# RWKV scan of a flow-matching layer: two lanes of five chunks become two lanes of four and a third one of two

## The chip, the cores and the metric

The kernel runs on one core of a Trainium2 chip, in one launch. The metric is the device time of one execution in microseconds (us). The core has a matrix engine (PE), which reads its work in one fixed order, a vector engine (DVE), an activation engine (ACT), a general engine (POOL) and a queue (SP) that issues every DMA of this kernel. Matrix products are written to eight PSUM banks, from which DVE and ACT fetch them.

## The reference

One layer for two requests: 512 tokens of a sample and 128 tokens of a prompt. Input projection, then latent attention (8 heads) beside RWKV-7 time mixing (16 heads of 64), one output projection, a norm, a SwiGLU network and a second norm. The part that the change touches is the scan, which runs once forward and once backward, over the sample from given states and over the prompt from zero:

```python
def step(S, inp):
    r_t, w_t, k_t, v_t, kk_t, a_t = inp
    sa = jnp.einsum("bhvk,bhk->bhv", S, -kk_t)
    S = S * w_t[:, :, None, :] + sa[..., None] * (kk_t * a_t)[:, :, None, :] + v_t[..., None] * k_t[:, :, None, :]
    return S, jnp.einsum("bhvk,bhk->bhv", S, r_t)
```

and the adaLN modulation, which multiplies SiLU of two condition vectors by a matrix `w_mod` of 2048 x 12288:

```python
m = jax.nn.silu(cond) @ w_mod + b_mod
return jnp.split(m[:, None, :], 6, axis=-1)
```

## The kernel before

All 640 tokens lie side by side in the free dimension, 512 of the sample and then 128 of the prompt. The scan is cut into ten chunks of 64 tokens (`C`, `NCH`). Within a chunk it is a set of matrix products; from chunk to chunk a state of 64 x 64 for each head goes on. Heads are taken in pairs (`npairs` is 8), one head in each half of the 128 partitions.

A pair needs both directions over all ten chunks. It is done in two halves (`j` = 0, 1). In each half two **lanes** run side by side: the forward lane over five chunks and the backward lane over the other five. Each pair and half, sixteen in all and here called a phase, goes through the same stations, written as generators:

- `rwkv_prep` multiplies keys and receptances by the decays into `nk` and `pr` (DVE, POOL).
- `rwkv_grams` forms, for each chunk and head, the Gram product of `pr` and `nk`: one product of 64 x 128 weights a head, ten chunks in groups of four, four and two. ACT copies its quarters to `mab` and `mrb`, DVE masks the others into `pr` and, once at the end, `mrb`.
- `rwkv_turned`, a side job, turns the values `v` (one copy `vr` reversed in time) into `sv` and `zv` with 64 x 64 products against the identity, and `nk` into `bk`.
- `inverse` inverts the triangular 64 x 64 blocks of `mab`, mostly on DVE.
- `rwkv_chain` runs five **steps**. A step has four kinds of PE run: `px` (rows `m<-sv,pr`), copied to `xs` by ACT; the outputs of the step before (`m<-pr,sv` and `m<-mrb,zv`); `psg` (`m<-xs,uf`), copied to `zv` by ACT for one head and by DVE for the other; and `pn` (`m<-zv,bk`), which DVE turns into the next chunk's state with one SCALAR_TENSOR_TENSOR a lane and head (`sv<-m,dc,sd`; `sd` comes from POOL). The next `px` reads these states.

A prompt of two chunks is the head or the tail of a lane, so the lanes end, start or hand over in mid-chain; the table `AFTER` says where each state goes.

PE's order is not left to a scheduler. Every generator above, and the work that fills the gaps, is a `Job` with a rank; `Jobs.step` keeps a modelled PE clock, lets the job of the lowest rank that is ready issue, and a job that yields a number (`HOP["x"]`, `HOP["s"]`, `HOP["p"]` in the chain) is ready again after so much modelled time. The scan has rank 0. Below it stand the modulation products (`wmods`, rank 2), and the input projection (`main`, rows `acc<-xh,whi` and the like) or, when that has ended, attention. They fill what the scan leaves free. The other engines' order is chosen when the program is built.

The modulation columns that are not needed at once come through `wmod_ahead`: a megabyte of `w_mod` is loaded into the one buffer `wm4`, and four products (rows `x<-wm,cs`, 128 x 32 weights, 512 columns, four column groups of PE) are issued back to back; after `HOP["wm"]` the next four follow.

Of the kernel before, what the change touches and what calls it, by code (L numbers as in the profile page):

```python
# [46 lines left out]
for _n, _w in (("ident", 128), ("gmask", 128), ("lmask", 32), ("par", 2), ("blk", 128), ("cen", 128), ("blk2", 2), ("sel", 2),  # L47
               ("ones", 1), ("rst", 320), ("rot", 128)):
    CST[_n] = (_off, _w)
    _off += _w  # L50
# [110 lines left out]
def step_kernel(ctx: ExitStack, tc: tile.TileContext, a: dict, o: dict, upto: int = 99, npairs: int = NPAIR, dbg=None):  # L161
# [33 lines left out]
    def half(name):  # L195
        return rtile(name, HN, "h", 1)

# [209 lines left out]
    def token_shift(p0, p1, mi, mk=edge):  # L407
# [12 lines left out]
        return ((slice(0, NS), s[:, :NS]), (slice(NS, NT), s[:, 513:641]))  # L420
# [260 lines left out]
    def nat(d, j):  # L681

        h = j if d == 0 else 1 - j
        return slice(h * HN, h * HN + HN)

    def view(t, d, j):
        v = t[:, nat(d, j)]
        return v if d == 0 else v[:, ::-1]
# [25 lines left out]
    HV = [slice(0, HN), slice(HN, NT)]  # L714

    def rwkv_decays(i, j, sh):
# [3 lines left out]
        for d in range(2):  # L720
            col = 8 * d + i
            both = [(t, lw[:, c0 + d * P: c0 + d * P + P], x, r_, b, mps()) for t, c0, x, r_, b in
                    ((ld, 0, xw, slice(0, 64), w0_h), (ta, 256, xa, slice(64, 128), a0_h))]
            for t, w, x, r_, b, ps in both:
                T.matmul(ps[:, :HN], w, x[:, nat(d, j)], start=True, stop=False)

            for t, w, x, r_, b, ps in both:
                T.matmul(ps[:, :HN], w[r_], xl[r_, nat(d, j)], start=False, stop=True, share=0.5)
            for t, w, x, r_, b, ps in both:
                od = t[:, HV[d]] if d == 0 else t[:, HV[d]][:, ::-1]  # L730
                act(od, ps[:, :HN], AF.Tanh, bias=b[:, col: col + 1], scale=0.5)
            yield 2 * HOP["dec"]
        ts(V, ld, ld, -0.5 * EXPH, -0.5 * EXPH)
        for v_ in HV:
            V.tensor_tensor_scan(out=ld[:, v_], data0=con("rst"), data1=ld[:, v_], initial=0.0, op0=ALU.mult, op1=ALU.add)
# [6 lines left out]
        for d in range(2):  # L742
            stt(nb[:, HV[d]], ta[:, HV[d]], 1.0, view(kk, d, j), ALU.add, ALU.mult)
        ts(V, ta, ta, ka_h[:, i: i + 1], ka_c[:, i: i + 1])
        for d in range(2):
            tt(V, ta[:, HV[d]], ta[:, HV[d]], view(k, d, j), ALU.mult)
        for d in range(2):
            n_ = ks[:, nat(d, j)]
            src = ta[:, HV[d]] if d == 0 else ta[:, HV[d]][:, ::-1]
# [6 lines left out]
    def rwkv_prep(i, j, sh, u):  # L756
# [5 lines left out]
        for h in range(2):  # L762
# [3 lines left out]
            for d in range(2):  # L766
                es = slice(5 * d, 5 * d + 5)
                kv_, rv_ = (ch(t[rh, nat(d, j)]) for t in (kk, r))
                if d == 1:
                    kv_, rv_ = kv_[:, ::-1, ::-1], rv_[:, ::-1, ::-1]  # L770
                tt(V, pr[h][rh, es, 0, 1:C], kv_[:, :, 1:C], dd5[rh, es, 0:C - 1], ALU.mult)
                A.copy(pr[h][rh, es, 0, 0:1], kv_[:, :, 0:1])
                tt(G, pr[h][rh, es, 1, :], rv_, dd5[rh, es, :], ALU.mult)
        yield HOP["prep"] + (FIRST[1] if i + j == 0 else 0.0)

    def rwkv_turned(i, j, sh, u):

        nk, v = u["nk"], sh["v"]
        vr = half("vr")
        A.copy(vr, view(v, 1, j))  # L780
        sv_, zv, bk = u["sv"], u["zv"], u["bk"] = wide("sv"), wide("zv"), wide("bk")
        yield HOP["vr"]
        for d in range(2):
            src = v[:, nat(0, j)] if d == 0 else vr
            es = slice(5 * d, 5 * d + 5)
            ps = mps()
            for c in range(5):
                for h in range(2):
                    T.matmul(ps[hrow(h), cc(c)], src[rows(h), cc(c)], ident[rows(h), rows(h)], start=True, stop=True)
            for h in range(2):  # L790
                A.copy(sv_[hrow(h), es, h, :], ch(ps[hrow(h), :HN]))
                A.copy(zv[hrow(h), es, h, :], ch(ps[hrow(h), :HN]))
            yield HOP["tv"]
# [7 lines left out]
    def rwkv_grams(u):  # L801

        nk, pr = u["nk"], u["pr"]
        mab, mrb = u["mab"], u["mrb"] = ch(slot("mab")), ch(slot("mrb"))
        for e0, n in EG:
            es = slice(e0, e0 + n)
            both = [mps(), mps()]
            for e in range(n):

                for h, ps in enumerate(both):  # L810
                    T.matmul(ps[:, e * P: e * P + P], nk[rows(h), e0 + e].rearrange("p b t -> p (b t)"),
                             pr[h][rows(h), e0 + e].rearrange("p b t -> p (b t)"), start=True, stop=True, share=0.5)
            for h, ps in enumerate(both):
                ps4 = ps[:, :n * P].rearrange("p (c b t) -> p c b t", b=2, t=C)
                q = 1 - h
                A.copy(mab[rows(h), es], ps4[rows(h), :, 0, :])
                tt(V, pr[h][rows(q), es].rearrange("p c b t -> p c (b t)"),
                   ps4[rows(q)].rearrange("p c b t -> p c (b t)"),
                   con("gmask")[rows(q)].unsqueeze(1).broadcast_to([C, n, P]), ALU.mult)
                A.copy(mrb[rows(h), es], ps4[rows(h), :, 1, :])  # L820
            yield 2 * HOP["gram"]
        tt(V, mrb, mrb, con("gmask")[:, C:].unsqueeze(1).broadcast_to([P, NCH, C]), ALU.mult)
# [4 lines left out]
    AFTER = {(0, 0): ("next", "next", "next", "next", "carry"), (0, 1): ("next", "final", "next", "next", "carry"),  # L827
             (1, 0): ("next", "next", None, "next", "final"), (1, 1): ("next", "next", "next", "next", None)}

    def rwkv_chain(i, j, sh, u):  # L830

        sv_, zv, bk, mrb, pr, dc, cy = u["sv"], u["zv"], u["bk"], u["mrb"], u["pr"], u["dc"], sh["carry"]

        def lanes(t, h, e):

            return t[rows(h), e: e + 6: 5, h, :]
# [4 lines left out]
        if j == 0:  # L841
            sh["fs"] = rtile("fs", 2 * C, "fs", 2)
            sh["y"] = slot("y")
        for h in range(2):
            if j == 0:
                for d, e in ((0, 0), (1, 7)):
                    DMA.dma_start(out=sv_[rows(h), e, h, :], in_=a["states"][d, i, rows(h)])
                G.memset(sv_[rows(h), 5, h, :], 0.0)
            else:
                G.tensor_copy(lanes(sv_, h, 0), lane2(cy, h))  # L850
                G.memset(sv_[rows(h), 3, h, :], 0.0)
        y = sh["y"]

        def outputs(c):


            pss = [mps()[:, :C] for _ in range(2)]
            ms = (slice(0, C), slice(None, None, -1))
            for d, ps in enumerate(pss):
                for h in range(2):  # L860
                    T.matmul(ps[rows(h)], sv_[:, 5 * d + c, h, :], pr[h][:, 5 * d + c, 1, :][:, ms[d]], start=True, stop=False)
            for d, ps in enumerate(pss):
# [1204 lines left out]
```

## Time and profile before

| | us |
|---|---|
| median of 3 runs (lowest, highest) | 3418.34 (3415.4, 3426.62) |
| the profiled execution | 3418.1 |
| its span, first to last instruction | 3416.3 |
| scan, first Gram product to last output written | 207.7 to 1428.9 |
| last attention output written | 1433.0 |

| engine | busy us | share |
|---|---|---|
| PE | 3231.4 | 95% |
| DVE | 2489.4 | 73% |
| ACT | 1447.3 | 42% |
| POOL | 994.2 | 29% |

Up to 1434 us the scan is interleaved with the projection and then with attention; from there on only the output projection and the network run, which the change does not touch. In the rows of the profile "x8" counts records: a product in plain fp32 leaves two of them, one in the rounded format of the projections (fp32r) one. L115 is the one line through which nearly all products are issued, so groups are told apart by their tiles, written out<-in.

### The profile page before, as it was taken

The page shows a single profiled execution, that of the slowest core. Times are in us where ns is not written, and L with a number is a line of the kernel's source. Part 1 is how long each engine was busy: PE and PEld are TensorE (multiplying, and loading weights), DVE is VectorE, ACT ScalarE, POOL GpSimd, SP SyncE. Part 2 cuts the span into 40 slices and gives each one's busy share as a digit, 9 for nine tenths or more (in the row PEclk, how much of TensorE's full clock was granted, in tenths as well). Part 3 has the DMA queues.
Part 4 walks back from the last instruction along what each step waited for, and adds up shares of the span by engine and source line. Part 5 has one row for each costly group of instructions (what it writes and reads, how often), then busy time and mean ns, then how long its engine had stood idle before and what let it go on. Part 6 is the DMA issues. An engine that isn't in the chain of part 4 may idle for free.

```text
span 3416.3 us, 71056 instructions
## 1 busy us (share of the span) xinstructions
PE 3231.4 (95%) x27746; PEld 2973.9 (87%) x27746; DVE 2489.4 (73%) x4469; ACT 1447.3 (42%) x3028; POOL 994.2 (29%) x1034
## 2 busy tenths in 40 slices
PE   7999998999997988899989999999999999999998
PEld 3777777777876777799989999999999999999997
DVE  2466675666658666568688888888887769999677
ACT  1344343444444545445454444444444444333234
POOL 0012222222222222112265444444442332222124
PEclk9999998999998999999989999999999999999998
DMA  9755454542222110275434443344444367888643
GB/s 359 241 185 166 145 171 142 158 151 94 66 63 84 44 34 28 79 246 173 145 108 154 149 139 124 127 141 135 130 123 121 114 218 278 298 286 285 214 142 119
DMA packets 289344, 527.71 MB, mean 154 GB/s; under 512 B 30512, under 2 KB 76272, under 8 KB 289008
## 3 DMA queue, kind: packets, MB, share of 16 engines
q1 hardware_dynamic: 289008, 523.18, 46.7%
q8 instruction: 217, 3.56, 0.4%
q14 instruction: 119, 0.97, 0.1%
HBM read 428.99 MB, written 92.44 MB: 153 GB/s over the span
## 4 chain that ended last, share of the span: by engine, by line
PE 65%; DVE 8%; ACT 3%; issue 2%; DMA 2%; POOL 2%; SPq 0%; ACTq 0%; DVEq 0%; POOLq 0%
PE b L115 51%; PE acc L115 7%; PE m L115 5%; PE x L115 1%; DVE ql L229 1%; DVE pr L229 1%; POOL z L229 1%; DVE z L229 1%; DVE ip L229 1%; ACT z L241 0%; DMA z<-zd 0%; PE acc L119 0%; DMA k<-rkv 0%; DVE nk L238 0%; DVE wlo L229 0%
## 5 line engine op out<-in xcount | busy, mean ns | idle before, releaser
L229 DVE TENSOR_TENSOR ql<-raw,qh 128x512 fp32r<-128x512 f32 (+1 forms) x1064 | 888.6, 850 | 264.9 <-ACT qh L1307 250.6
L1307 ACT CAST qh<-raw 128x512 fp32r<-128x512 f32 (+1 forms) x1064 | 633.5, 610 | 831.0 <-PE b L115 643.2
L115 PE MATMUL b<-t,qh 128*128 128x320 f32 x2816 | 623.4, 310 | 8.3 <-ACT qh L1307 7.1
L229 POOL TENSOR_TENSOR raw<-raw,raw 128x512 f32<-128x512 f32 x240 | 351.8, 1466 | 807.1 <-DVE ql L229 561.2
L115 PE MATMUL b<-op,qh 128*128 128x320 f32 x2560 | 552.8, 311 | 2.0 <-DMA op<-hd 1.2
L115 PEld LDWEIGHTS b<-t,qh 128*128 128x128 f32 x2816 | 473.1, 189 | 9.6 <-ACT qh L1307 8.1
L115 PE MATMUL b<-p,qh 128*128 128x320 f32 x2112 | 469.5, 311 | 0.0
L115 PE MATMUL b<-t,ql 128*128 128x320 f32 x1408 | 436.2, 311 | 5.4 <-DVE ql L229 5.4
L115 PEld LDWEIGHTS b<-op,qh 128*128 128x128 f32 x2560 | 425.8, 189 | 4.0 <-ACT qh L1307 1.9
L115 PE MATMUL b<-op,ql 128*128 128x320 f32 x1280 | 378.9, 311 | 5.6 <-DVE ql L229 5.5
L115 PEld LDWEIGHTS b<-p,qh 128*128 128x128 f32 x2112 | 356.9, 190 | 0.1
L115 PE MATMUL b<-p,ql 128*128 128x320 f32 x1056 | 329.4, 312 | 6.1 <-DVE ql L229 6.1
L115 PE MATMUL acc<-xh,whi 128*128 128x320 f32 x1056 | 265.2, 333 | 9.7 <-ACT P L1170 3.9
L115 PEld LDWEIGHTS b<-t,ql 128*128 128x128 f32 x1408 | 265.3, 189 | 7.3 <-DVE ql L229 7.3
L115 PE MATMUL acc<-xh,wlo 128*128 128x320 f32 x1056 | 264.6, 333 | 4.8 <-DVE wlo L229 4.8
L115 PE MATMUL acc<-xl,whi 128*128 128x320 f32 x1056 | 261.5, 330 | 0.5 <-DVE xl L229 0.5
L115 PEld LDWEIGHTS b<-op,ql 128*128 128x128 f32 x1280 | 236.7, 189 | 8.4 <-DVE ql L229 8.2
L115 PE MATMUL b<-mh,qh 128*128 128x320 f32 x1024 | 230.2, 314 | 7.0 <-ACT qh L1307 6.0
L115 PEld LDWEIGHTS acc<-xh,whi 128*128 128x128 f32 x1056 | 180.8, 197 | 33.5 <-issue 12.7
L115 PEld LDWEIGHTS b<-p,ql 128*128 128x128 f32 x1056 | 200.1, 190 | 8.5 <-DVE ql L229 8.5
L229 DVE TENSOR_TENSOR wlo<-raw,whi 128x512 fp32r<-128x512 f32 (+1 forms) x161 | 110.3, 686 | 124.0 <-ACT whi L266 115.4
L115 PEld LDWEIGHTS acc<-xh,wlo 128*128 128x128 f32 x1056 | 180.6, 196 | 22.6 <-issue 9.2
(330 smaller groups left out, 5465.1 us busy)
## 6 DMA issues: line engine op xcount, KB each, us to landing
wm<-in_w_mod_dram SPq DMA_DIRECT2D x64, 1024.0 KB, 5.4
raw<-in_w_gate_dram SPq DMA_DIRECT2D x188, 256.0 KB, 2.7
raw<-in_w_up_dram SPq DMA_DIRECT2D x188, 256.0 KB, 2.9
op<-hd SPq DMA_DIRECT2D x136, 320.0 KB, 5.3
wm<-in_w_mod_dram SPq DMA_DIRECT2D x64, 512.0 KB, 7.5
raw<-in_w_out_dram SPq DMA_DIRECT2D x128, 256.0 KB, 2.9
raw<-in_w_down_dram SPq DMA_DIRECT2D x128, 256.0 KB, 5.4
raw<-in_w_in_dram SPq DMA_DIRECT2D x127, 256.0 KB, 2.7
```

The lines of the kernel that those rows point to most:

```text
L115: self.eng.matmul(out, lhsT, rhs, start=start, stop=stop)
L229: eng.tensor_tensor(out=out, in0=x, in1=y, op=op)
L1307: A.copy(hi, x)
```

## The change

- **Tokens are laid out anew** for the scan: the first 256 of the sample, the 128 of the prompt, the last 256 of the sample. A half `j` now has a segment of six chunks and one of four (`SEG`, `CHS`), one forward and one backward.
- **Three lanes, four steps.** In each half the two sample lanes take four chunks each, and the prompt's two chunks are a third lane that runs only in the first two steps (`lanes`). The products of all lanes of a step, outputs too, share one bank. ACT and DVE copy the third lane's part of `zv` with an instruction of its own each.
- **Gram products on quarters**: for each chunk and head two products with 64 x 64 weights in place of one with 64 x 128, sorted so that the quarters that go to `mab` and `mrb` for both heads lie in one bank; one ACT copy and one masked DVE copy fetch them.
- **Values move**: the reversed copy is made in `rwkv_prep`, and the turning of `v` follows the second and third Gram group at once instead of coming from the side job. The initial states are loaded in the side job.
- **Modulation** loads two megabytes into two buffers and issues eight products back to back, then waits 1.5 times as long. The space comes from a reserved area of on-chip memory that is cut to 1024 bytes.

The core of the diff:

```diff
     def wmod_ahead(n):
-        for k in range(0, KT, 4):
-            raw = hp.tile([P, 2048], F32, tag="wm4", name=nm("wm4"), bufs=1).rearrange("p (k c) -> p k c", k=4)
-            DMA.dma_start(out=raw, in_=a["w_mod"][n, k: k + 4].rearrange("k p c -> p k c"))
-            yield HOP["wm"]
-            for j in range(4):
-                yield raw[:, j]
+        for k in range(0, KT, 8):
+            raws = []
+            for q in (k, k + 4):
+                raw = hp.tile([P, 2048], F32, tag="wm4", name=nm("wm4"), bufs=2).rearrange("p (k c) -> p k c", k=4)
+                DMA.dma_start(out=raw, in_=a["w_mod"][n, q: q + 4].rearrange("k p c -> p k c"))
+                raws += [raw[:, j] for j in range(4)]
+            yield 1.5 * HOP["wm"]
+            yield from raws
...
+    SEG = (slice(0, 384), slice(384, NT))
+    CHS = (slice(0, 6), slice(6, NCH))
...
+        vr = u["vr"] = rtile("vr", 384, "h", 1)
+        A.copy(vr[:, :SEG[1 - j].stop - SEG[1 - j].start], sh["v"][:, SEG[1 - j]][:, ::-1])
...
+        sv_, bk = u["sv"], u["bk"]
+        for h in range(2):
+            if j == 0:
+                for d, q in ((0, 0), (1, 6)):
+                    DMA.dma_start(out=sv_[rows(h), q, h, :], in_=a["states"][d, i, rows(h)])
+                G.memset(sv_[rows(h), 4, h, :], 0.0)
+            else:
+                G.tensor_copy(sv_[rows(h), 2:7:4, h, :], cy[rows(h)].rearrange("p (d v) -> p d v", v=C))
+                G.memset(sv_[rows(h), 0, h, :], 0.0)
...
+        def values(g):
...
-                for h, ps in enumerate(both):
-                    T.matmul(ps[:, e * P: e * P + P], nk[rows(h), e0 + e].rearrange("p b t -> p (b t)"),
-                             pr[h][rows(h), e0 + e].rearrange("p b t -> p (b t)"), start=True, stop=True, share=0.5)
-            for h, ps in enumerate(both):
-                ps4 = ps[:, :n * P].rearrange("p (c b t) -> p c b t", b=2, t=C)
-                q = 1 - h
-                A.copy(mab[rows(h), es], ps4[rows(h), :, 0, :])
-                tt(V, pr[h][rows(q), es].rearrange("p c b t -> p c (b t)"),
-                   ps4[rows(q)].rearrange("p c b t -> p c (b t)"),
-                   con("gmask")[rows(q)].unsqueeze(1).broadcast_to([C, n, P]), ALU.mult)
-                A.copy(mrb[rows(h), es], ps4[rows(h), :, 1, :])
+                for h in range(2):
+                    for b in range(2):
+                        T.matmul(both[b != h][rows(b), e * P: e * P + P], nk[rows(h), e0 + e, b, :],
+                                 pr[h][rows(h), e0 + e].rearrange("p b t -> p (b t)"), start=True, stop=True, share=0.33)
+            pa, pb = (ps[:, :n * P].rearrange("p (c b t) -> p c b t", b=2, t=C) for ps in both)
+            A.copy(mab[:, es], pa[:, :, 0, :])
+            for h in range(2):
+                q = rows(1 - h)
+                tt(V, pr[h][q, es].rearrange("p c b t -> p c (b t)"), pb[q].rearrange("p c b t -> p c (b t)"),
+                   con("gmask")[q].unsqueeze(1).broadcast_to([C, n, P]), ALU.mult)
+            tt(V, mrb[:, es], pa[:, :, 1, :], con("gmask")[:, C:].unsqueeze(1).broadcast_to([P, n, C]), ALU.mult)
+            if n_:
+                values(n_ - 1)
             yield 2 * HOP["gram"]
-        tt(V, mrb, mrb, con("gmask")[:, C:].unsqueeze(1).broadcast_to([P, NCH, C]), ALU.mult)
...
+        def lanes(e):
+
+            return [q + e for q in first] + ([(4, 0)[j] + e] if e < 2 else [])
...
-        for e in range(5):
+
+        for e in range(4):
+            qs_ = lanes(e)
             px = mps()
-            for d in range(2):
+            for l, q in enumerate(qs_):
...
+            xs = rtile("xs", 3 * C, "xs", 2)
+            A.copy(xs[:, :len(qs_) * C], px[:, :len(qs_) * C])
...
             psg = mps()
-            for d in range(2):
+            for l, q in enumerate(qs_):
                 for h in range(2):
-                    T.matmul(psg[rows(h), cc(d)], u["u"][rows(h), cc(5 * d + e)], xs[rows(h), cc(d)], start=True, stop=True)
-            A.copy(lanes(zv, 0, e), lane2(psg, 0))
-            V.tensor_copy(lanes(zv, 1, e), lane2(psg, 1))
+                    T.matmul(psg[rows(h), cc(l)], u["u"][rows(h), cc(q)], xs[rows(h), cc(l)], start=True, stop=True)
+            A.copy(both(zv, 0, e), lane2(psg, 0))
+            V.tensor_copy(both(zv, 1, e), lane2(psg, 1))
+            if len(qs_) > 2:
+                A.copy(zv[rows(0), qs_[2], 0, :], psg[rows(0), cc(2)])
+                V.tensor_copy(zv[rows(1), qs_[2], 1, :], psg[rows(1), cc(2)])
             yield HOP["s"]
...
-                for d in ds:
-                    q = 5 * d + e
-                    dst = sv_[rh, q + 1, h, :] if to[d] == "next" else (cy if to[d] == "carry" else sh["fs"])[rh, cc(d)]
-                    stt(dst, pn[rh, cc(d)], dc[rh, q: q + 1], sd[rh, cc(d)], ALU.mult, ALU.add)
-            if e < 4:
+                for l in ls:
+                    dst = place(l, e)
+                    dst = dst[rh, h, :] if len(dst.shape) > 2 else dst[rh]
+                    stt(dst, pn[rh, cc(l)], dc[rh, qs_[l]: qs_[l] + 1], sd[rh, cc(l)], ALU.mult, ALU.add)
+            if e < 3:
                 yield HOP["p"]
...
-    nc = _bacc.Bacc("TRN2", target_bir_lowering=False, num_devices=1)
+    nc = _bacc.Bacc("TRN2", target_bir_lowering=False, num_devices=1, dynamic_dma_scratch_size=1024)
```

What the built programs hold, engine by engine, at three places. First PE, in the chain of half 0 of the second pair, from the products that end the outputs to the `pn` run (`m` is a PSUM tile, `xs`, `zv` and `bk` operands of the chain). Before, the third of five steps, with two lanes and one modulation burst of four:

```order
L115 MATMUL m_4467<-mrb_3762,zv_3952 64x64 x2
L115 MATMUL m_4468<-mrb_3762,zv_3952 64x64 x2
L115 MATMUL m_4479<-xs_4462,uf_162 64x64 x4
L115 MATMUL x_4006<-wm_750_4367,cs 32x512 x4
L115 MATMUL m_4492<-zv_3952,bk_3953 64x64 x4
```

The same chain after, the second of four steps:

```order
L115 MATMUL m_4509<-mrb_3822,zv_3819 64x64 x6
L115 MATMUL m_4525<-xs_4502,uf_162 64x64 x6
L115 MATMUL acc_4486<-xl_241,whi_4401 128x320 x2
L115 MATMUL acc_4486<-xh_240,wlo_4402 128x320 x2
L115 MATMUL acc_4486<-xh_249,whi_4401 128x320 x2
L115 MATMUL x_4162<-wm_725_4370,cs 32x512 x4
L115 MATMUL x_4162<-wm_726_4372,cs 32x512 x4
L115 MATMUL m_4552<-zv_3819,bk_3820 64x64 x6
```

Each run of the chain has six products in place of four in this step, and two modulation bursts stand together. Counted over the whole order up to the output projection, PE goes from a product on the full array (128 x 128 weights) to one on a part of it 388 times before and 319 times after. By the kind that follows: modulation bursts 64 and 47, values 27 and 0, runs of the chain 153 and 132, all others 144 and 140.

Second, DVE in the chain of half 0 of the third pair, from one copy of `zv` over the state updates (`sv`) to the next. Before:

```order
L900 COPY zv_5778<-m_6199 64x2x64
L238 SCALAR_TENSOR_TENSOR sv_5777<-m_6214,dc_5213,sd_6192 64x64 x4
L900 COPY zv_5778<-m_6253 64x2x64
L229 TENSOR_TENSOR wlo_6267<-raw_6171,whi_6266 128x512
L238 SCALAR_TENSOR_TENSOR sv_5777<-m_6274,dc_5213,sd_6238 64x64
```

After:

```order
L226 TENSOR_TENSOR wlo_6345<-raw_6217,whi_6344 128x512
L235 SCALAR_TENSOR_TENSOR sv_5653<-m_6310,dc_5329,sd_6269 64x64 x6
L235 SCALAR_TENSOR_TENSOR us_6330<-t_6329,mu_h,us_6330 128x641
L915 COPY zv_5654<-m_6386 64x2x64
L918 COPY zv_5654<-m_6386 64x64
L235 SCALAR_TENSOR_TENSOR sv_5653<-m_6405,dc_5329,sd_6365 64x64 x2
```

Six state updates stand together where four stood, and the third lane adds a copy of `zv` of its own (L918) behind that of the two sample lanes (L915).

Third, DVE at the end of the third pair's half 1 and the start of the fourth pair's half 0 (`pr` products of `rwkv_prep`; `y` are the chain's outputs). Before:

```order
L238 SCALAR_TENSOR_TENSOR sv_6691<-m_7303,dc_6040,sd_7273 64x64 x4
L229 TENSOR_TENSOR y_6178<-m_7328,y_6178 128x64
L229 TENSOR_TENSOR y_6178<-m_7329,y_6178 128x64
L900 COPY zv_6692<-m_7340 64x2x64
L229 TENSOR_TENSOR wlo_7408<-raw_7245,whi_7407 128x512
L238 SCALAR_TENSOR_TENSOR fs_6177<-m_7355,dc_6040,sd_7325 64x64 x2
L229 TENSOR_TENSOR pr_7374<-kk_6741,D_7029 64x5x63 x2
L229 TENSOR_TENSOR pr_7375<-kk_6741,D_7029 64x5x63 x2
L229 TENSOR_TENSOR y_6178<-m_7360,y_6178 128x64
L229 TENSOR_TENSOR y_6178<-m_7361,y_6178 128x64
```

After:

```order
L235 SCALAR_TENSOR_TENSOR sv_6581<-m_7403,dc_6195,sd_7363 64x64 x4
L226 TENSOR_TENSOR pr_7465<-kk_6872,D_7128 64x6x63
L226 TENSOR_TENSOR pr_7465<-kk_6872,D_7128 64x4x63
L226 TENSOR_TENSOR y_6259<-m_7426,y_6259 128x64 x2
L915 COPY zv_6582<-m_7437 64x2x64
L226 TENSOR_TENSOR pr_7466<-kk_6872,D_7128 64x6x63
L226 TENSOR_TENSOR pr_7466<-kk_6872,D_7128 64x4x63
L226 TENSOR_TENSOR y_6259<-m_7452,y_6259 128x64 x2
```

Two of the four `pr` products have moved ahead of the last step's `zv` copy, and the other two stand right behind it, so that fewer follow the end of the chain.

More of the change, by code (lines that the diff above doesn't have):

```diff
@@ L719, in rwkv_decays @@
         ld, ta = slot("ld"), slot("ta")
-        for d in range(2):
+        for g, sg_ in enumerate(SEG):
+            d = g ^ j
+            w_ = sg_.stop - sg_.start
             col = 8 * d + i
@@ L765, in rwkv_prep @@
             tt(V, nk[rh, :, 1 - h, :], ch(ta)[rh], ch(ld)[rh], ALU.mult)
[L766 to L769, printed above, removed]
+            for g, es in enumerate(CHS):
+                kv_, rv_ = (ch(t[rh, SEG[g]]) for t in (kk, r))
+                if g != j:
                     kv_, rv_ = kv_[:, ::-1, ::-1], rv_[:, ::-1, ::-1]
@@ L773, in rwkv_prep @@
                 tt(G, pr[h][rh, es, 1, :], rv_, dd5[rh, es, :], ALU.mult)
+        vr = u["vr"] = rtile("vr", 384, "h", 1)
+        A.copy(vr[:, :SEG[1 - j].stop - SEG[1 - j].start], sh["v"][:, SEG[1 - j]][:, ::-1])
         yield HOP["prep"] + (FIRST[1] if i + j == 0 else 0.0)
     def rwkv_turned(i, j, sh, u):
[L778 to L793, printed above, removed]
+        nk, cy = u["nk"], sh["carry"]
+        sv_, bk = u["sv"], u["bk"]
[7 more added lines that the diff above has]
+                G.memset(sv_[rows(h), 0, h, :], 0.0)
+        yield 0.4
         for e0, n in EG:
@@ L841, in rwkv_chain @@
+        gap = first[1] - first[0]
         if j == 0:
@@ L843, in rwkv_chain @@
             sh["y"] = slot("y")
[L844 to L859, printed above, removed]
+        y, fs = sh["y"], sh["fs"]
@@ new lines, in lanes, with both, lane2, place @@
+        def lanes(e):
+            return [q + e for q in first] + ([(4, 0)[j] + e] if e < 2 else [])
+        def both(t, h, e):
+            return t[rows(h), first[0] + e: first[1] + e + 1: gap, h, :]
+        def lane2(t, h):
+            return t[rows(h), :2 * C].rearrange("p (d v) -> p d v", v=C)
+        def place(l, e):
+            if l == 2:
+                return sv_[:, lanes(e)[2] + 1] if e == 0 else fs[:, cc(j)]
+            if e < 3:
+                return sv_[:, lanes(e)[l] + 1]
+            return cy[:, cc(1 - l)] if j == 0 else None
@@ L860, in outputs @@
+        def outputs(e):
+            qs_ = lanes(e)
+            ps = mps()
+            turned = [(q >= 6) != j for q in qs_]
+            for l, q in enumerate(qs_):
                 for h in range(2):
-                    T.matmul(ps[rows(h)], sv_[:, 5 * d + c, h, :], pr[h][:, 5 * d + c, 1, :][:, ms[d]], start=True, stop=False)
-            for d, ps in enumerate(pss):
+                    T.matmul(ps[rows(h), cc(l)], sv_[:, q, h, :], pr[h][:, q, 1, :][:, ::-1 if turned[l] else 1],
+                             start=l == 0, stop=False)
+            for l, q in enumerate(qs_):
@@ L863, in outputs @@
                 for h in range(2):
-                    T.matmul(ps[rows(h)], zv[rows(h), 5 * d + c, h, :], mrb[rows(h), 5 * d + c, :][:, ms[d]], start=False, stop=True)
-            for d in range(2):
-                yc = y[:, nat(d, j)][:, cc(c if d == 0 else 4 - c)]
+                    T.matmul(ps[rows(h), cc(l)], zv[rows(h), q, h, :], mrb[rows(h), q, :][:, ::-1 if turned[l] else 1],
+                             start=False, stop=l == len(qs_) - 1)
+            for l, q in enumerate(qs_):
+                c = q if not turned[l] else 15 - q if q >= 6 else 5 - q
+                yc = y[:, cc(c)]
@@ L955, in rwkv_post @@
             yield HOP["gup"]
-        DMA.dma_start(out=mix_d[8 + i], in_=y)
+        for out, src in ((slice(0, 256), slice(0, 256)), (slice(256, NS), slice(384, NT)), (slice(NS, NT), slice(256, 384))):
+            DMA.dma_start(out=mix_d[8 + i][:, out], in_=y[:, src])
     def rwkv():
```

108 lines of the change are left out of this document (55 added, 53 removed).

## The prediction

> **What bounds the kernel now.** First the chain of work that ended last, in its shares by engine, then the busy time by stage (columns: stretch, its length, busy PE, PEld, DVE, ACT, POOL with records, granted PE clock, DMA share, GB/s):
>
> ```profile
> PE 65%; DVE 8%; ACT 3%; issue 2%; DMA 2%; POOL 2%; SPq 0%; ACTq 0%; DVEq 0%; POOLq 0%
> ```
>
> ```profile
> 200.00:1050.00 850.00, 794.35 (x9698) 651.47 (x9698) 550.15 (x1211) 356.79 (x908) 190.53 (x324) 0.96 0.41 130
> 1050.00:1434.00 384.00, 334.69 (x3980) 290.91 (x3978) 261.78 (x600) 187.10 (x469) 93.75 (x141) 0.94 0.12 38
> 1434.00:1770.00 336.00, 309.05 (x1984) 300.25 (x1985) 253.33 (x410) 169.42 (x327) 101.10 (x87) 0.93 0.59 179
> ```
>
> The scan runs in the first two of these stretches. PE is busy there for 794 of 850 us (93%) and 335 of 384 us (87%); DVE for 65% and 68%. What follows 1434 us is untouched work behind the same fence, so the change is worth what it takes from the 1234 us of the scan. Which waits interrupt PE there, in total over that stretch (engine, tile, what it waits for: us, times, longest):
>
> ```profile
> PE m L115 <- DVE y L229: 22.1, 19, 2.7
> PE x L115 <- DVE ev L360: 8.1, 3, 6.1
> PE m L115 <- DVE zv L900: 6.5, 4, 4.1
> PE m L115 <- ACT pm L635: 6.3, 6, 2.7
> PE m L115 <- POOL sv L851: 6.0, 6, 1.2
> PE acc L115 <- ACT P L1170: 5.7, 4, 2.5
> PE m L115 <- DVE sv L238: 5.0, 2, 4.6
> ```
>
> Nothing large stands out: `zv`, `sv` and `xs`, the hand-overs within a chain, cost a few us over 80 steps. The gaps of the scan are filled by projection, modulation and attention, so **PE's own work sets the time**, and a shorter chain of latencies is worth little by itself. The terms below are therefore stretches of PE's row, from start to start.
>
> One step, near the middle of the first stretch, shows what a run costs (start, us, engine, line, out<-in, weights, shape, records):
>
> ```profile
> 571.10 0.56 PE L115 MATMUL acc<-xh,wlo 128*128 128x320 f32 x2
> 571.50 0.46 PE L115 MATMUL acc<-xh,whi 128*128 128x320 f32 x2
> 571.80 0.46 PE L115 MATMUL acc<-xl,whi 128*128 128x320 f32 x2
> 572.09 0.45 PE L115 MATMUL acc<-xh,wlo 128*128 128x320 f32 x2
> 572.48 0.45 PE L115 MATMUL m<-zv,bk 128*64 128x64 f32 x8
> 572.86 0.56 PE L115 MATMUL acc<-xh,whi 128*128 128x320 f32 x2
> ...
> 573.93 0.49 PE L115 MATMUL m<-sv,pr 128*64 128x64 f32 x8
> 574.22 0.44 PE L115 MATMUL m<-pr,sv 128*64 128x64 f32 x8
> 574.59 0.45 PE L115 MATMUL m<-mrb,zv 64*64 64x64 f32 x8
> 574.87 0.41 PE L115 MATMUL m<-xs,uf 64*64 64x64 f32 x8
> 575.21 0.42 PE L115 MATMUL acc<-xh,whi 128*128 128x320 f32 x1
> ```
>
> **1. Fewer alternations: −13.8 us.** A pair of projection records takes 0.295 us in the middle of a run (571.50 to 572.09 is two pairs in 0.59). The run of four pairs from 571.10 to 572.48 takes 1.38, not 4 x 0.295 = 1.18: going from the full array to a part of it and back costs 0.20 us. The order has 388 such changes before and 319 after: 69 x 0.20 = 13.8. This is pure PE time, beside nothing. Bounds: 0 if the 0.20 is a wait that merely moves, 13.8 if it is the array's.
>
> **2. Chain runs: −2.6 us.** A dropped step takes with it `px` 0.29 (573.93 to 574.22), outputs 0.37 + 0.28, `psg` 0.34 and `pn` 0.38: 1.66 us. For it ten runs (five kinds, two steps) grow from 8 records to 12. A record in a long run is read from the turning of values, 20 records in 0.73 us to the next run, against 8 in 0.28 for `m<-mrb,zv` above: 0.45 / 12 = 0.0375.
>
> ```profile
> 598.46 0.80 PE L115 MATMUL m<-cst,v 64*64 64x64 f32 x20
> 599.19 1.07 PE L115 MATMUL x<-wm,cs 128*32 128x512 f32 x8
> 600.18 0.80 PE L115 MATMUL m<-cst,vr 64*64 64x64 f32 x20
> ```
>
> So 10 x 4 x 0.0375 = 1.50 comes back: −0.16 a phase, −2.6 over 16. The records' number is the same in both kernels, so the bounds are 0 and, with half the runs' starts free, about −10.
>
> **3. Modulation bursts of eight: −3.2 us.** A burst of four products shows 8 records in two waves: the second starts 0.45 us after the first (568.75, 569.20), the next run 0.55 us after that (569.75).
>
> ```profile
> 568.75 1.07 PE L115 MATMUL x<-wm,cs 128*32 128x512 f32 x8
> 569.20 0.61 PE L115 MATMUL x<-wm,cs 128*32 128x512 f32 x4
> 569.75 0.51 PE L115 MATMUL m<-sv,pr 128*64 128x64 f32 x7
> 607.68 1.07 PE L115 MATMUL x<-wm,cs 128*32 128x512 f32 x8
> wm<-in_w_mod_dram SPq DMA_DIRECT2D x64, 1024.0 KB, 5.4
> ```
>
> Two bursts take 2 x 1.00 us; one of 16 records takes three waves at 0.45 and one at 0.55, 1.90: 0.10 saved, 32 times for the 64 loads of the last row. What could take it back is the load. One megabyte lands 5.4 us after its issue (last row: issues, size, median us to landing); of two, issued together when the burst before has freed both buffers, I estimate that the second lands some 3 us later, as they share the same engines. Bursts started as little as 8.5 us apart (599.19 to 607.68), of which the modelled wait is now half as long again, so that about 12 us lie between them and 1.9 + 5.4 + 3 fit. If one burst in three came 1 us late, it would be +10: bounds −3.2 and +10.
>
> **4. The third lane's waits: +9.6 us.** State updates follow one another on DVE, and `px` needs the last of them:
>
> ```profile
> 573.04 0.99 DVE L238 SCALAR_TENSOR_TENSOR sv<-m,dc,sd 64x64 f32<-64x64 f32 x4 [1.24 <-PE m L115]
> 571.22 0.26 ACT L899 COPY zv<-m 64x128 f32<-64x128 f32 x1
> 571.51 0.29 DVE L900 COPY zv<-m 64x128 f32<-64x128 f32 x1 [1.58 <-ACT zv L899]
> ```
>
> Four take 0.99, 0.25 each, and end at 574.03, when `px` (573.93) has begun: its last products already stand right behind the last update, with no slack. The modelled wait `HOP["p"]` ahead of `px` is as before. After step 0 there are six updates: +0.50, less 0.15 by which the longer `pn` (4 x 0.0375, counted in 2) pushes `px` back too: 0.35. After step 1 one update of the prompt stands ahead of the last that `px` needs: 0.25. Sum 0.60 a phase, 9.6 over 16. Behind a waiting `px` everything on PE is queued, so it is lost in full. Bound below: 0, if DVE starts on the first bank's products earlier.
>
> The third lane's `zv` adds a copy on ACT and one on DVE, and in these rows DVE's copy is released by ACT's of the same bank (571.22 + 0.26, start 571.51). If the two new ones follow in turn, that is 0.26 + 0.29 = 0.55 us more. `zv` is complete at 571.80 here and `pn` starts at 572.48: 0.68 us of projection products hides it, and I count it at 0. If that cover is gone it costs 0.55 x 2 steps x 16 = +17.6 (rival B), so the term's upper bound is +27.
>
> **5. DVE at the pair's end: −7.5 us.** Of the 22.1 us that PE waits for `y`, the Gram runs hold part:
>
> ```profile
> L115 PE MATMUL m<-pr,nk 64*128 64x128 f32 x640 | 55.4, 292 | 14.0 <-DVE y L229 7.5 <-POOL sv L851 6.0 <-ACT mrb L820 0.4
> 353.00 3.77 DVE L229 TENSOR_TENSOR pr<-kk,D 64x315 f32<-64x315 f32 x4
> 356.80 0.36 DVE L229 TENSOR_TENSOR y<-m,y 128x64 f32<-128x64 f32 x2
> 357.17 0.57 PE L115 MATMUL m<-pr,nk 64*128 64x128 f32 x5 [1.66 <-DVE y L229]
> ```
>
> Four `pr` products of the next pair, 3.77 us, stand on DVE between the chain's last update and its last `y`; the next Gram needs the banks that `y` holds and waits 1.66 us. All such waits are the 7.5 us of the group's row. In the new order two of the four products stand ahead of the last `zv`, and 3.77 / 2 = 1.9 us is more than 1.66, so the wait goes; next late there is POOL, whose 6.0 us stay. Bounds −7.5 and 0.
>
> **6. Gram products on quarters: 0.** A group of four chunks, 16 records, takes 1.09 us (585.92 to 587.01 below), 0.068 a record. The change doubles the records, each with weights of half the width.
>
> ```profile
> 585.92 1.16 PE L115 MATMUL m<-pr,nk 64*128 64x128 f32 x16
> 587.01 0.56 PE L115 MATMUL acc<-xl,whi 128*128 128x320 f32 x2
> ```
>
> If four quarters run side by side as two halves do now, 32 records take the time of 16 before. The nearest row is the turning of values, 64 x 64 products as well: 0.0375 a record, 32 of them 1.2 against 1.09, less by one change of kind. I take 0, as it is near that row. If only half of that runs side by side, each chunk costs (1.09 − 0.20) / 4 = 0.22 more, 160 chunks +35.
> The Trainium skill ("TensorEngine Tiling (Array Packing)", section "Restrictions and Gotchas", Gotcha 1) says that different row tiles cannot access the same PSUM bank simultaneously. Sorted quarters put both heads, that is both row halves, into one bank; by that rule they would take turns, and the sum would be +35 us higher (rival C). The trace speaks against it so far: `m<-cst,v` writes one bank from both halves and has 0.0375 us a record.
>
> **Covered.** ACT loses some 35 us of copies and DVE gets about 50 instructions more; ACT at 42% and DVE at 65% are hidden by PE, apart from term 4. Values moved into the Gram station are the same products on PE. The smaller reserved area gives only space.
>
> **Sum.** −13.8 − 2.6 − 3.2 + 9.6 − 7.5 + 0 = −17.5 us. The profiled execution took 3418.1 us, its span 3416.3; it lies 0.2 under the median of the runs shown (3418.34). From 3418.1: **3401 us**.
>
> **Rivals.** *A, the scan's path sets the end.* A step less saves 573.93 − 569.75 = 4.18 us of latency in each of 16 phases, 66.9, less 9.6: 3361. For it: 50 us idle in the second stretch. Against it: PE is 93% busy in the first, and the order ends the scan a few rows ahead of the last attention product. 6%.
> *B, the third lane's `zv` takes the place of what is gained.* No projection stands where its copies wait: −17.5 + 17.6, 3418, no change. It decides where less than 0.68 us of other products stands between the sample lanes' `zv` and `pn`. For it: ACT and DVE take turns on a bank in the row above. 20%.
> *C, Gram quarters take turns*, two at a time instead of four: 32 records at 0.068. Slower, 3401 + 35 = 3436. Half of that price, 0.051 a record, is where the gain is gone. Against it: the turning of values. 10%.
> *D, two megabytes come late*, more than the bound of term 3: also slower: with 1 us late in each of 32 bursts 3401 + 3 + 32 = 3436. 2%.
>
> **How the numbers follow.** Forecast 62%, A 6, B 20, C 10, D 2. About 0.3%, 10.3 us, is what a measurement of this kernel can tell from no change. Forecast bounds: with 1 at half its size, 4 at 17 instead of 9.6 and 5 at 0 the sum is +4; with 4 at 0 and 2 at its bound it is −34.5, 3422 and 3384 us. Of the forecast's 62, 52 are faster by over 10.3, 9 within, 1 slower; A is faster; of B 18 are within and 2 slower; C and D are slower. Faster 0.58, same 0.27, slower 0.15. The range takes in the forecast's own bounds with a little below them, B, and the part of C and D short of their full price: 3380 to 3434.
>
> **What would show it.** Step 1: shorter stretches of PE with the same waits; about 14 us fewer busy. 2 and 4: `px` of the second and third step starts behind the last of six and five updates, 0.35 and 0.25 us idle. 3: sixteen records in 1.90 us, none waiting for the load. 5: `y` gone from the waits of the Gram runs. 6: 32 records of a Gram group in 1.1 us; 2 us would be C. B would show as `pn` waiting for the third lane's copies. Wrong altogether would be an end of the scan set by a wait that the profile of before does not have.

## The result, and the profile after

The changed kernel takes 3387.34 us (median of 4 runs, 3386.45 to 3391.81) against 3416.87 us of the kernel before on the same chip: a ratio of 0.9914, 95% interval 0.9888 to 0.9939. That is 29.5 us less, where 17.5 were forecast; 3401 was predicted with a range of 3380 to 3434, so it lies inside, on the fast side. Run again beside the experiments, the changed kernel gave 3384.58 us, ratio 0.9910 (0.9894 to 0.9926).

First the busy time by stage of the changed kernel (columns as before). The stage that the change does not touch begins 34 us earlier (first product of the output projection at 1403.9 us instead of 1438.0) and takes 1982 us instead of 1978; over all runs it takes 1974 to 1983:

```profile
200.00:1050.00 850.00, 787.28 (x10442) 660.59 (x10438) 579.50 (x1305) 335.00 (x837) 210.87 (x348) 0.96 0.40 133
1050.00:1404.00 354.00, 310.97 (x3912) 276.41 (x3911) 238.17 (x562) 163.15 (x407) 90.43 (x137) 0.96 0.13 37
1404.00:1740.00 336.00, 311.51 (x2004) 302.84 (x2005) 254.65 (x412) 169.37 (x327) 101.20 (x88) 0.94 0.58 177
1740.00:3385.00 1645.00, 1622.30 (x10950) 1610.46 (x10948) 1339.30 (x2089) 679.32 (x1217) 590.80 (x440) 0.99 0.52 173
```

Then five groups of instructions on PE from 200 to 1404 us, whose idle time (last columns: us before them, and what ended it) the readings below use:

```profile
L115 PE MATMUL m<-pr,nk 64*64 64x128 f32 x1280 | 49.7, 277 | 12.8 <-DVE pr L226 10.6 <-DVE mrb L226 2.2
L115 PE MATMUL m<-sv,pr 128*64 128x64 f32 x640 | 43.1, 243 | 3.5 <-DVE sv L235 3.4
L115 PE MATMUL m<-zv,bk 128*64 128x64 f32 x576 | 37.4, 238 | 13.9 <-DVE zv L915 5.4 <-DVE zv L918 4.2 <-ACT zv L914 3.1
L119 PE MATMUL m<-cst,nk 128*128 128x128 f32 x160 | 27.0, 285 | 9.9 <-ACT bk L791 5.4 <-DVE ks L226 4.0 <-DVE y L963 0.4
L115 PE MATMUL x<-cst,ev 128*128 128x2 f32 x120 | 15.6, 252 | 1.3 <-DVE ev L359 1.3
```

and the same groups of the kernel before (200 to 1434 us; the Gram row is in the prediction):

```profile
L115 PE MATMUL m<-sv,pr 128*64 128x64 f32 x640 | 42.3, 244 | 5.1 <-DVE sv L238 5.0
L115 PE MATMUL m<-zv,bk 128*64 128x64 f32 x576 | 37.5, 241 | 8.0 <-DVE zv L900 6.5 <-DVE y L229 1.0 <-ACT zv L899 0.4
L119 PE MATMUL m<-cst,nk 128*128 128x128 f32 x160 | 26.4, 281 | 0.0
L115 PE MATMUL x<-cst,ev 128*128 128x2 f32 x120 | 16.2, 257 | 8.1 <-DVE ev L360 8.1
```

Waits have changed places: the copy of the modulation sums (`ev`) no longer holds PE, but `pn` waits 5.9 us more for `zv`, and the transposes that make `bk` (`m<-cst,nk`) wait 9.9 us where they waited for nothing. Groups that are not shown moved as much: `m<-u,pm` from 6.4 to 1.4 us, `acc<-kh,qh` from 6.3 to 1.1, `m<-ks,cst` from 0 to 5.0.

The busy times of these rows overlap one another on PE, and part of them ran at half the clock (140 us before the output projection in the trace of before, 110 in this one). So PE's work was also added up from its records' starts: from each record to the next one's start (or to its own end, where PE then idles), halved where the granted clock was 0.50, up to the output projection's first product. Beside it stand the time lost to the half clock and the idle time. Halving is a little too much: a projection pair takes 0.533 us at 0.50 and 0.294 at full clock, which makes some 1 us between two rows of the table. One profiled execution each, us:

```text
                          projection  modul.  Gram  chain  rest   work   lost at 0.50  idle
before                       530.4    107.7   51.1  138.3  411.7  1239.1     60.0      131.0
changed                      516.1    104.2   43.4  138.8  414.8  1217.4     47.3      131.4
changed, again (e1)          515.0    101.0   43.7  138.8  413.5  1212.1     51.6      131.8
Gram on halves (e2)          516.0    102.9   49.4  137.8  416.6  1222.7     46.0      129.2
bursts of four (e3)          517.4    107.4   42.8  138.8  415.3  1221.9     36.5      123.6
no third lane (e4)           526.2    101.8   47.9  140.6  412.6  1229.2     48.4      125.8
later px (e5)                517.8    102.8   42.4  133.4  416.2  1212.5     44.9      123.6
before, bursts of 8 (e9)     528.8    102.7   51.7  140.3  414.4  1237.8     46.9      120.0
later px, four (e12)         516.6    108.7   42.3  129.9  416.1  1213.7     45.2      135.2
```

"Chain" is the five kinds of chain run. The columns projection, Gram and chain repeat within about 1 us between two executions of the changed kernel, modulation within some 3. PE's work falls by 21.7 and 27.0 us, 24 on average, and the idle time stays. In the first pair of traces work, half clock and idle time together fall by 34 us. The 12.7 us less at half clock in the first pair of traces are hardly the change's: the profiled execution of before had a mean clock of 0.969, below its usual one. Over 43 runs of the kernel before (one more, at a clock of 0.866, is left out as disturbed) and 8 of the changed one the mean granted clock is the same, 0.972.

### The profile page after: what moved, and what is told of

Same layout as the page of the kernel before. It is cut to its first block, busy times and chain, and to the rows that moved or that the text cites. A ratio compares the mean times of both kernels' runs of the same rounds, so it can differ in the third digit from the quotient of the medians.

```text
span 3385.6 us, 72312 instructions
## 1 busy us (share of the span) xinstructions
PE 3198.5 (94%) x28386; PEld 2964.2 (88%) x28386; DVE 2486.0 (73%) x4520; ACT 1398.1 (41%) x2890; POOL 1006.4 (30%) x1050
## 4 chain that ended last, share of the span: by engine, by line
PE 73%; DVE 11%; DMA 3%; ACT 3%; issue 3%; POOL 1%; SPq 0%; ACTq 0%; DVEq 0%; POOLq 0%
PE b L115 51%; PE acc L115 11%; PE m L115 8%; PE x L115 2%; DVE z L226 1%; DVE pr L226 1%; DMA wm<-in_w_mod_dram 1%; DVE ql L226 1%; DVE wlo L226 1%; DMA k<-rkv 1%; DVE ip L226 1%; POOL z L226 1%; PE acc L119 0%; DVE nk L226 0%; ACT z L238 0%
## 5 line engine op out<-in xcount | busy, mean ns | idle before, releaser
L115 PE MATMUL acc<-xh,wlo 128*128 128x320 f32 x1056 | 256.7, 325 | 3.2 <-DVE wlo L226 3.2
L263 ACT CAST whi<-raw 128x512 fp32r<-128x512 f32 (+1 forms) x161 | 95.8, 595 | 246.8 <-PE acc L115 197.3
```

The source lines that it names most:

```text
L115: self.eng.matmul(out, lhsT, rhs, start=start, stop=stop)
L263: A.copy(hi, r)
```

## The experiments

Each is compared with the changed kernel's ratio to the kernel before, 0.9910 (0.9894 to 0.9926), by its own ratio; 0.001 is 3.4 us.

**e1, the changed kernel again.**

> The changed kernel once more, to compare the next three with on one chip. The gain over the kernel before is 29.5 us by the medians (17.5 forecast). If part of it is the granted clock (110 us at half speed before the scan's end here, 137 in the kernel before), another profile of the same kernel may show 120 to 140 us at half speed and a time some 5 to 10 us longer. If the stretches at half speed belong to the program, it shows about 110 again.

Measured 3384.58 us. Half speed before the scan's end: 124 us, against 110 in the first execution. The stretches vary from one execution to the next, so a single pair of traces doesn't tell the clock's share.

**e2, the Gram products on halves again.**

```diff
-                    for b in range(2):
-                        T.matmul(both[b != h][rows(b), e * P: e * P + P], nk[rows(h), e0 + e, b, :],
-                                 pr[h][rows(h), e0 + e].rearrange("p b t -> p (b t)"), start=True, stop=True, share=0.33)
+                    T.matmul(both[h][:, e * P: e * P + P], nk[rows(h), e0 + e].rearrange("p b t -> p (b t)"),
+                             pr[h][rows(h), e0 + e].rearrange("p b t -> p (b t)"), start=True, stop=True, share=0.528)
```

> The changed kernel with the Gram products as one of 64 x 128 weights a head again (the banks then hold one head each, so ACT and DVE fetch the diagonal quarters with two copies instead of one); the order on PE is as in the changed kernel otherwise. If the quarters are worth what the starts on PE show (52 us of pitch before, 43 after), 6 to 12 us slower than the changed kernel. If they cost nothing, as the prediction had it, the same within 3 us. If they take turns by the bank, faster by up to 35 us.

Measured 3386.43 us, ratio 0.9919 (0.9905 to 0.9934): 3 us slower by the ratios, with an uncertainty of some 6. In the table the Gram column rises by 5.9 us. PE's timeline, first a group on quarters in the changed kernel, then one on halves in e2 (start, us, ..., records):

```profile
504.49 0.46 PE L115 MATMUL acc<-xh,wlo 128*128 128x320 f32 x2
504.87 1.92 PE L115 MATMUL x<-wm,cs 128*32 128x512 f32 x16
506.73 1.10 PE L115 MATMUL m<-pr,nk 64*64 64x128 f32 x32
507.66 0.86 PE L115 MATMUL m<-cst,v 64*64 64x64 f32 x24
```

```profile
654.60 1.16 PE L115 MATMUL m<-pr,nk 64*128 64x128 f32 x16
655.70 0.56 PE L115 MATMUL acc<-xh,wlo 128*128 128x320 f32 x2
```

32 records take 506.73 to 507.66, 0.93 us, where the values follow at once, and 1.03 us in the undisturbed groups that a projection product follows; 16 on halves take 1.09 to 1.10, whatever follows them, values or projection. Quarters of both heads that share a bank, each head's row half writing 64 partitions of its own there, do not take turns: the prediction's price for that was 0.22 us for each of four chunks, 0.88 us more. This is where the trace answers the rule on row tiles and PSUM banks that the prediction weighed ("TensorEngine Tiling (Array Packing)", "Restrictions and Gotchas", of the Trainium skill): for this pattern no such cost shows.

**e3, bursts of four from one buffer in the changed kernel** (the function `wmod_ahead` of before).

> The changed kernel with modulation bursts of four out of one buffer. By terms 1 and 3 of the prediction: 17 changes of kind more at 0.20 us and 32 x 0.10 us of waves, 6.6 us slower. If a change of kind costs nothing in the end, 0 to 3 us slower; if the second megabyte comes late in the changed kernel, faster.

Measured 3370.27 us, ratio 0.9877 (0.9859 to 0.9895): 11 us *faster* by the ratios and 14 by the medians. Faster had been expected only if the second megabyte came late, and it does not: PE waits for `wm` 1.3 and 0.0 us in the two traces of the changed kernel, and 5.2 us here. PE's work is 4.5 to 9.8 us more, as terms 1 and 3 have it, but 8 us less is idle and 11 to 15 us less is lost at half clock. The clock is no accident of one execution here: 0.977 to 0.979 in all four runs, 0.970 to 0.974 in the eight of the changed kernel.

**e4, the change without the third lane**: the kernel before, its Gram function's products and copies as in the change, bursts of eight. The new layout of the tokens and the moved values are missing with the lane.

> The kernel before (two lanes of five chunks, values turned by the side job) with the Gram products on quarters and the bursts of eight, so that the third lane alone is missing from the change. If PE's own work decides, it is slower than the changed kernel by what lanes save in changes of kind and runs: about 47 changes at 0.20 us and 2.6 us, less the waits, 5 to 15 us. If the scan's path sets the end, nearly the whole gain is in the lanes: 22 us or more.

Measured 3394.97 us, ratio 0.9948 (0.9931 to 0.9965): 10 to 13 us slower than the changed kernel. This is PE's own work: 11.8 to 17.1 us more in the table, 10 to 11 of it projection products, which stand in 361 runs here and in 288 there. How much of that is the lane's and how much the moved values' was not separated.

**e5, later `px`.**

```diff
-                yield HOP["p"]
+                yield HOP["p"] + (0.35, 0.25, 0.0)[e]
```

> The changed kernel with the modelled wait ahead of px longer by 0.35 us after step 0 and by 0.25 us after step 1, so that projection products are ordered into the waits for the six and five state updates. By term 4 of the prediction (9.6 us of such waits) some 5 to 10 us faster than the changed kernel; by the trace after (3.4 us of waits of px for sv) the same within 3 us.

Measured 3363.44 us, ratio 0.9855 (0.9836 to 0.9874), 19 to 21 us faster than the changed kernel and 1.45% faster than the kernel before: the lowest of all, though its interval overlaps that of e3. PE's timeline at the `px` after step 0 (12 records), first in e1, then in e5:

```profile
702.83 0.83 PE L115 MATMUL m<-sv,pr 128*64 128x64 f32 x11
703.39 0.27 PE L115 MATMUL m<-pr,sv 128*64 128x64 f32 x1
703.49 0.22 PE L115 MATMUL m<-sv,pr 128*64 128x64 f32 x1
```

```profile
702.72 0.45 PE L115 MATMUL acc<-xh,whi 128*128 128x320 f32 x2
703.11 0.57 PE L115 MATMUL m<-sv,pr 128*64 128x64 f32 x12
703.50 0.52 PE L115 MATMUL m<-pr,sv 128*64 128x64 f32 x12
```

From the first to the last record it is 0.66 us in e1 (to 703.49) and typically 0.35 in e5; after step 1, 0.49 and 0.23. So 0.31 + 0.26 = 0.57 us a phase is a wait for the last state update, 9.1 us over 16, and it hides *inside* the run: the column of idle time shows only 3.5 us for `px`. In the table the chain loses 5.4 us, and 3.4 of idle before `px` go as well: 8.8 us. But PE's whole work, 1212.5 us, is no less than in e1 (1212.1), as projection, modulation and the rest take more; against e1 it is idle time (8 us) and half clock (7 us) that fall. So the 9.1 us are shown in the `px` runs, not in the kernel's time.

**e6, the `pr` products segment by segment.** The loops over heads and segments change places in `rwkv_prep`.

> The changed kernel with the pr products on DVE written segment by segment instead of head by head, so that the first Gram group has all it needs after two or three of the four products. The Gram runs wait 10.6 us for pr in the changed kernel: if that wait is on the path that sets the time, 4 to 9 us faster; if something else is late next at the same place (y, POOL), the same within 3 us.

Measured 3386.21 us, ratio 0.9923 (0.9907 to 0.9940), the same or slightly slower. The Gram runs' wait fell from 12.8 to 6.8 us:

```profile
L115 PE MATMUL m<-pr,nk 64*64 64x128 f32 x1280 | 50.2, 277 | 6.8 <-DVE pr L226 5.3 <-DVE mrb L226 1.4
```

PE's whole idle time in the trace fell by 4.6 to 5.0 us, but not the time of the kernel. Six us at 6 places are below what this comparison tells.

**e7 and e8, an unused product among the projection's.**

```diff
             yield from mm3(ps, w, k * P, xs[kt], kt == 0, kt == len(xs) - 1)
+            if k == 1 and len(xs) == KT and g % 2 == 0:
+                T.eng.matmul(ps[0:64, 0, 400:464], ident[0:64, 0:64], con("ident")[0:64, 0:64], start=False, stop=False)
```

e8 has `ps[:, 0, 400:464], ident, con("ident")[:, 0:64]`. 56 such products each.

> The changed kernel with one unused fp32 product of 64 x 64 weights and 64 columns in every second granule of the input projection, between two projection products, into unused columns of their bank. In the trace the pitch around it is the cost of going to a part of the array and back: 0.20 us by term 1 beside its own two records. If the cost belongs to what stands around a chain run and not to the array, there is none here beyond its records (some 0.08 us).

> The same with 128 x 128 weights. If 0.20 us is for the array's division, the pitch around it has nothing beyond its own two records (some 0.08 to 0.15 us). If it is for the change of number format (fp32r to fp32), it is as large as with the 64 x 64 product.

PE's timeline, first e7, then e8:

```profile
656.23 0.46 PE L115 MATMUL acc<-xh,wlo 128*128 128x320 f32 x2
656.62 0.33 PE L287 MATMUL acc<-cst 64*64 64x64 f32 x2
656.88 0.56 PE L115 MATMUL acc<-xh,whi 128*128 128x320 f32 x2
657.27 0.46 PE L115 MATMUL acc<-xl,whi 128*128 128x320 f32 x2
```

```profile
653.23 0.46 PE L115 MATMUL acc<-xh,wlo 128*128 128x320 f32 x2
653.53 0.33 PE L287 MATMUL acc<-cst 128*128 128x64 f32 x2
653.66 0.54 PE L115 MATMUL acc<-xh,whi 128*128 128x320 f32 x2
654.04 0.46 PE L115 MATMUL acc<-xl,whi 128*128 128x320 f32 x2
```

From the projection pair ahead to the second pair behind, e7 takes 656.23 to 657.27, 1.04 us, and e8 653.23 to 654.04, 0.81. Both hold four projection records (0.59). So the product on a quarter costs 0.45 us and the one on the full array 0.22: **0.23 us is for going to a part of the array and back**. In 23 undisturbed places of each trace the two stretches take 1.04 and 0.80 to 0.81 us. Something also remains without any change to a part: in e8 the pair behind takes 0.38 instead of 0.295. I put that down to the change of number format (plain fp32 between fp32r products), which no run separates.
In the kernel's time the two can't be told apart: 3396.67 us, ratio 0.9954 (0.9938 to 0.9969), and 3399.68, 0.9964 (0.9953 to 0.9975). 56 x 0.23 would be 13 us, but not every product stands between undisturbed projection pairs: added up as in the table, PE's work is 7 us more in e7 than in e8, and its idle time 6 us less. e7's runs lie between 3388 us (clock 0.976) and 3407 (0.971).

**e9, bursts of eight alone in the kernel before.**

> The kernel before with the bursts of eight from two buffers alone (and the smaller reserved area). By terms 1 and 3 of the prediction 6 us faster than before. If bursts of eight lower the granted clock, as e1 and e3 suggest (0.973 against 0.978), 5 to 15 us slower than before at a clock some 0.003 to 0.005 lower, with 3 to 7 us less of time times clock.

Measured 3392.76 us, ratio 0.9940 (0.9922 to 0.9958): 20 us *faster*, where PE's whole work is only 1.3 us less. Modulation work falls by 5.0 us, 13 of 374 projection runs go, and 11 us of idle time, 6.6 of them the wait for `ev`:

```profile
L115 PE MATMUL x<-cst,ev 128*128 128x2 f32 x120 | 15.2, 249 | 1.5 <-DVE ev L362 1.5
```

So my idea after e3, that bursts of eight lower the clock, has fallen: it is 0.974 here on average, not below the 0.972 of before.

**e10, e11 and e12** ask whether it is the place where the modulation ends, and whether the two faster edits add up. e10 has `yield 2.05 * HOP["wm"]`, e11 bursts of four with the next megabyte loaded a burst ahead and `yield 0.75 * HOP["wm"]`, e12 the edits of e3 and e5 together.

> The changed kernel with the modelled wait ahead of a burst of eight 2.05 instead of 1.5 times as long, so that the modulation products end where they end with bursts of four (about 783 us instead of 648). If the place where they end decides (later phases then have modulation beside the projection, and fewer stretches of projection alone), as fast as with bursts of four, 3370 us, clock 0.977 or more. If the burst of eight itself lowers the clock, still 3385 us and 0.973.

> The changed kernel with bursts of four, 0.75 times the modelled wait and two buffers loaded one burst ahead, so that the modulation products end as early as in the changed kernel (about 650 us). If the place where they end decides, 3385 to 3390 us at a clock near 0.973; if the burst of eight does, near 3370 us at 0.978.

> The changed kernel with both edits that made it faster: bursts of four from one buffer, and the modelled wait ahead of px longer by 0.35 and 0.25 us. If they are independent, 14 and 21 us add to 3350 us; if both do the same (fewer stretches at half speed), near 3363 us. In time times clock 4 us less than with the bursts of four alone, or more.

Measured 3376.06 us (0.9896, 0.9876 to 0.9915), 3379.55 (0.9901, 0.9881 to 0.9921) and 3381.56 (0.9907, 0.9889 to 0.9925). The modulation's last product starts at 768 us in e10 and at 637 in e11 (648 in the changed kernel, 783 in e3). Both times lie between the two cases that they were to separate, and their intervals overlap those of both, so these runs don't tell whether the place or the burst decides. e12 is the plainest: it has e5's shorter chain (129.9 us) and PE does 8 us less than in e3, yet it is some 10 us slower than e3, with 12 us more idle and 9 more lost at half clock. Part of its idle time is back where the bursts of eight had removed it (`x<-cst,ev`, 8.5 us), the rest is spread over small waits.

## Why the prediction was right, step by step

**That PE's own work decides** held: the kernel gained 29.5 and 29.2 us at equal mean clock, PE's work fell by 24 on average, its idle time stayed at 131. For single edits it did not hold in time: e9 is 20 us faster than before with 1.3 us less work, and e3 faster than the changed kernel with more. That the latency of a chain is worth little held (rival A, 3361, did not come). From its first `px` to its last output a chain took 20.1 us in the median instead of 22.2 (18.4 to 32.0 instead of 20.4 to 32.6). In e4 it took 23.2: 3.1 us more than in the changed kernel, 50 over 16 phases, and the kernel was 10 to 13 us slower. In e9 it took 23.4, longer than before, and the kernel was 20 us faster.

**1, alternations (−13.8): right.** The projection lost 14.3 and 15.4 us; its runs fell from 374 to 288, so 0.17 to 0.18 us a run. The name of the price was only partly right: the 0.20 is what projection pairs lose around a foreign run, and around the product of e7 they lose as much, but around the full-array product of e8 they still lose 0.08 (medians of the 23 places). So part of it is not for going to a part of the array.

**2, chain runs (−2.6): right in sign, too small.** The chain's column hardly changed, because term 4 is inside it; with the waits taken out it is 133.4 (e5) and 129.9 (e12) against 138.3, −4.9 and −8.4. The first is used below.

**3, bursts (−3.2): right.** 16 records take 504.87 to 506.73, 1.86 us (1.90 forecast), and modulation fell by 3.5 and 6.7 us. The loads' median to landing rose from 5.4 to 7.2 us and PE waited 1.3 us for them, about as much as before (1.1). What was missed is the wait for `ev`, which goes with this edit (8.1 to 1.3 us; 1.5 in e9, but 4.2 and 8.5 in e3 and e12). It is not the size of the bursts that removes it: in e11, with bursts of four loaded ahead, it is 1.0.

**4, third lane's waits (+9.6): right**, 9.1 us by the length of the `px` runs in e1 and e5, though not as idle time ahead of `px`, where I had said it would show. Of rival B's price (17.6) 5.9 us came.

**5, DVE at the pair's end (−7.5): half right.** No Gram run waits for `y` any more, as forecast; the other large wait for `y`, of `m<-xa,lw`, stays (11.7 to 10.4 us). But I kept POOL's 6.0 us at half 1, and there it is now DVE's `pr` that is late (six waits of 0.8 to 1.4 us, 7.3 in all), and later Gram groups in attention wait another 5.5 us. Net 14.0 to 12.8, so −1.2.

**6, Gram on quarters (0): too high.** The column fell by 7.5 us. Quarters that a projection product follows save some 3 (e4's column beside that of before and of e9: 3.2 and 3.8). Another 3.3 come from the values right behind two groups of each phase, 0.10 us each (0.93 instead of 1.03), as they are 64 x 64 products too; halves gain nothing from them (1.09), so e2 shows both together as 6. Rival C is refuted.

**Moved values, and all else, at nothing: wrong.** The transposes for `bk` now wait 9.9 us. They don't in the two-lane kernels e4 and e9 (0.0), and do in each three-lane kernel looked at, so it came with what those two leave out, the lanes, the new layout or the moved values. Which of these it was, and so whether the values are to blame, was not separated.

**The 12 us by which the sum was short.** In the table's terms the forecast was 10.0 us less work (terms 1 to 4) and 7.5 less idle time (term 5). Measured is 24.5 us less work: 7.5 more from term 6, 5.3 from terms 1, 2 and 3 together, 4.2 because only 5.4 of term 4's 9.6 us lie inside runs, against 2.5 more for the rest. The idle time stayed: `ev` (−7) and smaller waits gave what `bk` (+9.9) and `zv` (+5.9) took, and term 5 brought 1.2. That makes 24.5 of the 29.5; the last 5 us are within the interval of the ratio (some 8 us to either side) and were not assigned. That the time lay inside the range is in part luck: term 6, counted at nothing, brought as much as term 5 was to bring and did not.

**What stays open** is what single edits are worth in time. Bursts of eight instead of four are worth −20 us in the kernel before, +14 in the changed one and −18 with the later `px` (e5 beside e12): about −8 on average, near the 6.6 us that terms 1 and 3 give, with a scatter twice as large as itself. The traces book that scatter under small waits (idle from 120 to 135 us) and under the half clock (36 to 60 us lost). What decides it was not found. Taken one edit at a time, bursts of eight alone (e9) would be two thirds of the gain, and by e3 they would be a loss. The changed kernel's gain over the one before stands by itself, but the shares of its parts can't be read from single edits in time; they were read from PE's work. That this work is the cause of the whole gain is therefore argued from the sums, and not shown edit by edit.

## What to carry to other kernels

Where one engine is 93% busy, count its work from start to start, at full clock, before and after: it repeats within a few us where the kernel's time scatters by twenty. A wait of a few tenths of a us inside a run of small products is not in the column of idle time; compare the run's length with an undisturbed run of as many records. And when instructions are ordered ahead of time, a new latency (six updates instead of four) asks for a longer modelled wait. It took the wait out of the `px` runs in both kernels that have it, but every such edit also moves everything else: with bursts of eight the kernel became 19 to 21 us faster, with bursts of four some 10 us slower (e12 beside e3).

## What the runs showed of the hardware

The mean granted clock can differ between two programs that are nearly alike: 0.977 to 0.979 in four runs of e3, 0.970 to 0.974 in eight of the changed kernel, which e3 differs from by the loading and the bursts of the modulation alone. Other programs spread more: 0.971 to 0.977 in six runs of e11. Within 43 runs of the kernel before, 0.001 of clock goes with 1.7 us of time. So a comparison of two traces should name both clocks. And 32 records (16 products) on quarters of the array, with both row halves writing one bank, each on partitions of its own, take 1.03 us where 16 records (8 products) on halves take 1.09.
